# Four pairs by seven products in the last two chunks of an up projection, with the fourth pair's left sums kept in HBM

## The chip, the cores and the metric

The kernel runs on one core of a Trainium2 chip. The metric is the device time of one execution in microseconds, the median of several runs. Beside the times there is a profile of one execution, taken by the hardware profiler.

## The reference

One decoder layer on 256 tokens of width 2048, in float32: a combined input projection, two groups of attention heads, an output projection with a norm and a residual, and then the part that matters here, an MLP with a squared ReLU and a hidden width of 8192:

```python
h = _rmsnorm(x, norm_mlp_pre[layer])
u = jnp.square(jax.nn.relu(h @ w_up[layer]))
x = x + _rmsnorm(u @ w_down[layer], norm_mlp_post[layer])
```

## The kernel before

**Products in three passes.** TensorE gets each float32 operand as two parts: `hi`, the value rounded by ScalarE (L306, L310 with a gain), and `lo`, the rest, by VectorE (L307, L311). A product is three matmuls (hi hi, hi lo, lo hi) of 128 x 128 by 128 x 512. All weights are loaded as `raw` tiles (five buffers) on SP's queue and split into `hi` and `lo` tiles (eight buffers). `Weights.get(i)` emits loads and splits up to six tiles ahead of the one that TensorE is about to use; four ahead around the norm. A load, a split or any other action can be hung in front of a tile by its index (`weights.first`).

**The up projection.** It goes by eight chunks of 1024 columns (`j`, 0 to 7). Within a chunk the 16 blocks of 128 rows (`k0` to `k15`) are taken in the steps of `UP_STEPS`. A step `k` takes one block: both token blocks by both halves of the columns, 12 matmuls. Two neighbouring blocks are a pair, and a pair can be computed by seven block products instead of eight (the Strassen-Winograd form): 21 matmuls instead of 24. This needs sums of the right-hand blocks (the weights) and of the left-hand blocks (the normed activations).

- A step `w` makes the weights' sums on VectorE (`seven`, L359 to L364): `t` and `u` from the two raw tiles in `ab`, which POOL loads; then four splits (b11, b, u, t).
- A step `p` takes weights' sums that were made ahead, by DMA alone, in HBM (`prepare`, L592 to L599): two copies on SP, three accumulating transfers on POOL, and a fourth. They go by the planning clock, one pair after another from 50 us of the plan on, 24 us of the plan for each pair. For chunks 1 to 4 the finished sums come back through POOL into the buffer `tu` (L433); from chunk 5 on, where `tu`'s place holds the output uT8, they come as raw tiles on SP's queue. `PREP` lists the pairs of all `p` steps.
- The left sums of pairs 0 to 3 are made once, in chunk 0 (`left_sums`, L1030 to L1041): pairs 0 to 2 lie in `st`, pair 3 in `st2`. The place of `st2` (tag uT10) is given to the output uT10 in chunk 5. So the first six chunks use four pairs, and chunks 6 and 7 three.

The seven products of all pairs add into the four accumulators of the chunk and into four more banks `m`. After the last pair, `close` (L1072, L1075) makes four closing sums from `m` in the buffer `c`, and `up_evac` adds each to its accumulator (L969) at the chunk's end, applies the ReLU with the norm's scale (`r`, L973), transposes on TensorE (`rt`, L300) and squares into uT (L991).

**Order.** Nothing is scheduled by the compiler. `Flow` keeps a planning clock, to which each matmul adds its expected duration (0.216 us). Chains of work off TensorE are generators that yield the delay until their next part; `flow.pump()`, called after every three matmuls, emits all parts that are due. The clock so fixes the order of instructions on every engine and queue; when they run is decided by semaphores. Each queue is in order: SP's holds raw loads, the stores of x (`xkeep`) and the preparations' copies; POOL's holds the norm's `rstd` operations (L517), the loads of `ab` and `tu`, and the accumulating transfers.

Around the norm between output and up projection (`residual`) the weights run four tiles ahead instead of six; afterwards the buffers are filled again while chunk 0 runs. The last chunk loads the raw tiles of its `w` steps through the five `raw` buffers (but for pair 0), since `ab` holds outputs by then.

Of the kernel before, what the change touches and what calls it, by code (L numbers as in the profile page):

```python
# [18 lines left out]
F32 = mybir.dt.float32  # L19
F32R = mybir.dt.float32r  # L20
# [6 lines left out]
P = 128  # L27
# [18 lines left out]
CW = 1024  # L46
# [50 lines left out]
NUP = FF // CW  # L97


def steps_of(text):  # L100

    return [(s[0], int(s[1:])) for s in text.split()]


UP_STEPS = {0: [("k", k) for k in range(KD)]}
for _j in range(1, 6):
    UP_STEPS[_j] = steps_of("k8 k9 k10 k11 p0 k12 w1 k13 p2 w3 k14 k15")
for _j in range(6, NUP):
    UP_STEPS[_j] = steps_of("k6 k7 k8 k9 k10 w0 k11 k12 w1 k13 w2 k14 k15")
SCALED = {j: range(8) for j in range(1, NUP)}  # L110
PREP = [(j, k) for j in UP_STEPS for w, k in UP_STEPS[j] if w == "p"]
D_PREP = (50.0, 24.0, 12.0)
# [151 lines left out]
def layer(nc, tc, io):  # L264
# [9 lines left out]
    dram = tc.alloc_tile_pool(name="dram", bufs=1, space=bass.MemoryType.DRAM)  # L274
# [69 lines left out]
    late = {}  # L344
# [35 lines left out]
    def seven_up(j, kp):  # L380
        def load():
            if j == FF // CW - 1 and kp:
                return [weights.load(up_weight(j, 2 * kp + i), CW, f"raw_w{j}_{kp}{i}") for i in range(2)]
            return load_two(late["ab"], nc.gpsimd, io["w_up"][2 * kp * P:(2 * kp + 2) * P, j * CW:(j + 1) * CW])

        return seven(load, lambda: [late["up"].tile([P, CW], F32, tag="T", bufs=2, name=f"{n}{j}_{kp}") for n in "tu"])
# [21 lines left out]
    def plan_seven(sums, fs, early, after, more=(), last=(), soon=False):  # L408

        at = max(len(weights.specs) - SUMS_AHEAD, after)  # L410
        if soon:
            more = (*more, (at - max(at - LOAD_AHEAD, after - 2), early))
        for n, f in (*more, (0, sums), *((0, f) for f in last)):
            weights.first.setdefault(at - n, []).append(f)
        return [weights.plan(f) for f in fs], len(weights.specs)
# [3 lines left out]
    wide_u, after, after_p = [], 0, 0  # L419
    for j in range(NUP):  # L420
        wide_u.append([])
        for what, k in UP_STEPS[j]:
            if what == "k":
                g = () if k in SCALED.get(j, ()) else (gcol[:, 8 + k:9 + k],)
                ts = [weights.plan(up_weight(j, k), 1, CW, *g)]
            elif what == "p":
                kept = sums_kept[j, k]
                srcs = [(up_weight(j, 2 * k)[:, :512], 512), (up_weight(j, 2 * k + 1), CW),
                        (kept[:, CW:], CW), (kept[:, :CW], CW)]
                if j < 5:  # L430
                    at = max(len(weights.specs) - 2 * LOAD_AHEAD, after_p)
                    weights.first.setdefault(at, []).append(
                        lambda kept=kept: nc.gpsimd.dma_start(out=late["tu"], in_=kept))  # L433
                    ts = [weights.plan(src, 1, n) for src, n in srcs[:2]] + [weights.plan(
                        lambda hi, lo, o=o: split(hi, lo, late["tu"][:, o:o + CW])) for o in (CW, 0)]
                    after_p = len(weights.specs)
                else:
                    ts = [weights.plan(src, 1, n) for src, n in srcs]
            else:
                ts, after = plan_seven(*seven_up(j, k), after, soon=j < NUP - 1 or k == 0)  # L440
            wide_u[j].append((what, k, ts))

    def down_weight(c, k):
# [14 lines left out]
    for c in range(2):  # L458
        wide_d.append([])
        for what, k in DOWN_STEPS[c]:  # L460
            if what == "k":
                ts = [weights.plan(down_weight(c, k), 1, CW)]
# [558 lines left out]
        tt(out=qs[:, 3], in0=fs[:, 2], in1=qs[:, 2], op=OP.subtract)  # L1021

    sums = []

    def left_sums(kp):

        up, k, tt = late["up"], 2 * kp, nc.vector.tensor_tensor
        f, q = [late["c"][:, i * 512:(i + 1) * 512] for i in range(2)]
        hs = [t[:, k:k + 2, :].rearrange("p k s -> p (k s)") for t in hT]
        tt(out=f, in0=hs[0].bitcast(F32), in1=hs[1].bitcast(F32), op=OP.add)  # L1030
        for i in range(2):
            nc.vector.tensor_scalar_mul(f[:, i * S:(i + 1) * S], f[:, i * S:(i + 1) * S], gcol[:, 8 + k + i:9 + k + i])
        four_sums(q, f)
        sp, i0 = (late["st"], 2 * kp) if kp < 3 else (late["st2"], 2 * kp - 6)
        st = [sp[:, i * 512:(i + 1) * 512] for i in (i0, i0 + 1)]
        yield 3.0
        for t, x in ((hs, f), (st, q)):
            nc.scalar.activation(t[0], x, AF.Copy)
        yield 1.5
        for t, x in ((hs, f), (st, q)):  # L1040
            tt(out=t[1], in0=x, in1=t[0].bitcast(F32), op=OP.subtract)  # L1041
        sums.append([[t[:, i * P:(i + 1) * P] for t in st] for i in range(4)])
        yield 0.5

    def some_sums(kps, after=0.0):
        yield after
        for kp in kps:
            yield from left_sums(kp)
# [20 lines left out]
    def close(c, m):  # L1069

        tt = nc.vector.tensor_tensor
        nc.scalar.activation(c[0], m[1], AF.Copy)  # L1072
        for out, x, y, op in ((1, m[6], c[0], OP.subtract), (2, m[7], c[1], OP.subtract),
                              (1, m[5], c[1], OP.add), (3, c[1], m[7], OP.subtract)):
            tt(out=c[out], in0=x, in1=y, op=op)  # L1075
        return dict(zip(PARTS, c))

    def closing():
        return [late["c"][:, i * 512:(i + 1) * 512] for i in range(4)]
# [3 lines left out]
    for j in range(FF // CW):  # L1083
        at = {bn: 4 * (j % 2) + i for i, bn in enumerate(PARTS)}
        if j == 0:
            accs = {bn: acc_bank(f"acc_u0_{bn[0]}{bn[1]}") for bn in at}
            at = {bn: (turn[0] - 3 + i) % 4 for i, bn in enumerate(at)}
        else:
            accs = {bn: bank(i, f"acc_u{j}_{bn[0]}{bn[1]}") for bn, i in at.items()}
        steps = wide_u[j]  # L1090
        order = in_order(len(steps), (APART[1], 0)) if j == 0 else [(t, b) for t, (w, _, _) in enumerate(steps)
                                                                    for b in range(NB if w == "k" else 1)]
        for t, b in order:
            what, k, tiles = steps[t]
            if (j, t, b) == (0, 8, 0):
                flow.finish(*res)
                late["po"].release()
                mix.release()
                late["up"] = pool("up", "right")
                late["st"] = late["up"].tile([P, 3 * CW], F32R, tag="st", bufs=1, name="st")  # L1100
                for n in ("ab", "c"):
                    late[n] = late["up"].tile([P, 2 * CW], F32, name=n)
                late["st2"] = late["up"].tile([P, CW], F32R, tag="uT10", bufs=1, name="st2")
                late["tu"] = late["up"].tile([P, 2 * CW], F32, tag="uT8", bufs=1, name="tu")
                flow.start(some_sums((0, 1)))
                flow.start(some_sums((2, 3), 18.0))
            if (j, t, b) == (FF // CW - 1, 4, 0):
                weights.limit -= 1
                u_next = split_u(0, 0)
            if what != "k":  # L1110
                flow.until(lambda: len(sums) > k)
            if what == "k":
                w = weights.get(tiles[0])
                h_done(k, b)
                for n in range(2):
                    c = slice(n * 512, (n + 1) * 512)
                    three(accs[b, n], [tok(hT[x], k, b) for x in range(2)], [w[x][:, 0, c] for x in range(2)], t == 0, t == len(steps) - 1)
                    if t == len(steps) - 1:
                        evac.append(flow.start(up_evac(2 * j + n, b, at[b, n], accs[b, n], 0.75 * (2 * b + n),
                                                       more[b, n] if j else None)))  # L1120
                    flow.pump()
                if b == NB - 1:
                    weights.free(tiles[0])
                continue

            pairs = [s[1] for s in steps if s[0] != "k"]
            first, last = k == pairs[0], k == pairs[-1]
            if first:
                m = {n: bank(i, f"m{n}_{j}") for n, i in zip((1, 6, 7, 5), free)}
            blocks = [[tok(hT[x], 2 * k + kk, bb) for x in range(2)] for kk, bb in ((0, 0), (1, 0), (1, 1))]  # L1130
            seven_products(tiles, (blocks, sums[k]), accs, m, first, last)
            if last:
                more = close(closing(), m)
        free = [at[bn] for bn in PARTS]
    u_last = evac[-4:]
# [197 lines left out]
```

## Time and profile before

| | |
|---|---|
| median of 3 runs | 1051.41 us (1051.28 to 1051.68) |
| the profiled execution | 1050.67 us; span 1048.9 us, mean granted TensorE clock 0.998 |
| TensorE matmuls (PE) | 1036.4 us busy, 4844 instructions |
| weight loads into TensorE (PEld) | 863.1 us |
| VectorE (DVE) | 810.6 us |
| ScalarE (ACT) | 633.0 us |
| GpSimd (POOL) | 98.9 us |
| HBM | read 244.18 MB, written 39.32 MB |

A row of the timeline has the start in us from the span's start, the duration, the engine, the line of the kernel, the operation, the tile that it writes and those that it reads, the shape and a count, and in brackets the idle time just before it with what ended it. SPq is SyncE's DMA queue. A row `x3` is several operations merged. A row of the waits has the total in us, the count and the longest. A row of the stretches has for each engine the busy time and the number of instructions.

### The profile page before, as it was taken

The numbers are of one execution on the slowest core, as the hardware profiler recorded it, in microseconds if no ns is written. First come the engines' busy times: TensorE is split into PE (matmuls) and PEld (weight loads), VectorE is DVE, ScalarE is ACT, GpSimd is POOL, SyncE is SP. The second block draws the span as 40 slices with busy tenths as digits, with TensorE's granted clock in tenths as the row PEclk, the third lists the DMA queues.
The fourth block names the chain that finished last, engine by engine and source line by source line (L and its number), as shares of the span: only waits on it lengthen the run. The fifth ranks groups of instructions, "written<-read, shape, count | busy, mean of one in ns | idle before, by whom it ended". The sixth has DMA issues, their size and how long they took to land.

```text
span 1048.9 us, 13584 instructions
## 1 busy us (share of the span) xinstructions
PE 1036.4 (99%) x4844; PEld 863.1 (82%) x4844; DVE 810.6 (77%) x1083; ACT 633.0 (60%) x846; POOL 98.9 (9%) x156
## 2 busy tenths in 40 slices
PE   9999999999999999999999999999999999999996
PEld 7888899888888788888888888888888888888885
DVE  6776546567557669988889798887899988989995
ACT  6675436565545466666756766656567564766661
POOL 0011111112111000010100000000000001112100
PEclk9999999999999999999999999999999999999999
DMA  9999879699878295766766656469778767788952
GB/s 298 369 298 298 221 197 321 197 258 300 227 219 259 84 362 180 281 207 241 262 214 222 228 191 212 139 227 322 249 272 312 267 226 260 264 301 318 368 196 81
DMA packets 93572, 260.81 MB, mean 249 GB/s; under 512 B 8768, under 2 KB 13376, under 8 KB 92096
## 3 DMA queue, kind: packets, MB, share of 16 engines
q1 hardware_dynamic: 71776, 190.61, 52.9%
q0 software_dynamic: 21152, 68.69, 23.0%
q8 instruction: 38, 0.62, 0.2%
q10 hardware_dynamic: 576, 0.64, 0.2%
q14 instruction: 30, 0.25, 0.1%
HBM read 244.18 MB, written 39.32 MB: 270 GB/s over the span
## 4 chain that ended last, share of the span: by engine, by line
PE 87%; DVE 6%; DMA 3%; issue 2%; ACT 2%; POOL 0%; DVEq 0%; POOLq 0%; SPq 0%; ACTq 0%
PE y L296 26%; PE acc_u L296 17%; PE acc_o L296 8%; PE m L296 6%; PE md L296 5%; PE acc_qk L296 4%; PE acc_v L296 4%; PE acc_cq L296 2%; PE acc_ukv L296 2%; PE acc_q L296 2%; PE acc_k L296 2%; DMA raw<-in_w_up 2%; DVE lo L307 2%; PE acc_uq L296 2%; PE acc_ckv L296 1%
## 5 line engine op out<-in xcount | busy, mean ns | idle before, releaser
L307 DVE TENSOR_TENSOR lo<-raw,hi 128x1024 fp32r<-128x1024 f32 (+3 forms) x241 | 269.7, 1137 | 96.3 <-ACT hi L306 95.5
L306 ACT ACTIVATE hi<-raw 128x1024 fp32r<-128x1024 f32 (+3 forms) x241 | 234.7, 988 | 98.0 <-PE y L296 21.5
L296 PE MATMUL y<-hi,uhi 128*128 128x512 f32 x376 | 146.7, 390 | 0.0
L296 PE MATMUL y<-hi,ulo 128*128 128x512 f32 x376 | 146.3, 389 | 0.0
L296 PE MATMUL y<-lo,uhi 128*128 128x512 f32 x376 | 146.3, 389 | 0.0
L296 PE MATMUL acc_u<-hi,hT_hi 128*128 128x512 f32 x356 | 141.7, 398 | 0.0
L296 PE MATMUL acc_u<-hi,hT_lo 128*128 128x512 f32 x356 | 139.2, 391 | 0.4 <-DVE hT_lo L307 0.4
L296 PE MATMUL acc_u<-lo,hT_hi 128*128 128x512 f32 x356 | 138.8, 390 | 0.0
L311 DVE SCALAR_TENSOR_TENSOR lo<-raw,gcol,hi 128x1024 fp32r<-128x1024 f32 x72 | 90.6, 1280 | 16.2 <-ACT hi L310 15.8
L310 ACT ACTIVATE hi<-raw,gcol 128x1024 fp32r<-128x1024 f32 x72 | 81.6, 1149 | 20.3 <-DMA raw<-in_w_up 12.8
L296 PEld LDWEIGHTS y<-hi,ulo 128*128 128x128 f32 x376 | 70.6, 188 | 14.8
L296 PEld LDWEIGHTS y<-hi,uhi 128*128 128x128 f32 x376 | 70.6, 188 | 14.6
L296 PEld LDWEIGHTS y<-lo,uhi 128*128 128x128 f32 x376 | 70.6, 188 | 14.4
L296 PEld LDWEIGHTS acc_u<-hi,hT_lo 128*128 128x128 f32 x356 | 66.8, 188 | 15.0 <-DVE hT_lo L307 0.8
L296 PEld LDWEIGHTS acc_u<-lo,hT_hi 128*128 128x128 f32 x356 | 67.0, 188 | 12.9
L296 PEld LDWEIGHTS acc_u<-hi,hT_hi 128*128 128x128 f32 x356 | 66.9, 188 | 12.9
L296 PE MATMUL m<-hi,st 128*128 128x512 f32 x156 | 56.5, 389 | 0.0
L296 PE MATMUL acc_o<-hi,mixT_hi 128*128 128x512 f32 x128 | 51.8, 405 | 0.0
L307 DVE TENSOR_TENSOR lo<-st_down,hi 128x1024 fp32r<-128x1024 f32 x40 | 48.0, 1220 | 3.9 <-ACT hi L306 3.8
L296 PE MATMUL acc_o<-hi,mixT_lo 128*128 128x512 f32 x128 | 50.2, 392 | 0.0
L296 PE MATMUL acc_o<-lo,mixT_hi 128*128 128x512 f32 x128 | 50.0, 390 | 0.0
L306 ACT ACTIVATE hi<-st_down 128x1024 fp32r<-128x1024 f32 x40 | 42.1, 1052 | 10.8 <-PE y L296 9.4
(331 smaller groups left out, 2037.6 us busy)
## 6 DMA issues: line engine op xcount, KB each, us to landing
raw<-in_w_down SPq DMA_DIRECT2D x88, 512.0 KB, 5.8
raw<-in_w_up SPq DMA_DIRECT2D x86, 512.0 KB, 4.6
raw<-in_w_in SPq DMA_DIRECT2D x55, 512.0 KB, 6.5
raw<-in_w_out SPq DMA_DIRECT2D x32, 512.0 KB, 7.3
ab<-in_w_up POOLq DMA_DIRECT2D x28, 512.0 KB, 5.1
sums<-in_w_up SPq DMA_DIRECT2D x20, 512.0 KB, 7.9
ab_down<-in_w_down POOLq DMA_DIRECT2D x20, 512.0 KB, 6.3
tu<-sums POOLq DMA_DIRECT2D x8, 1024.0 KB, 5.1
```

Source lines behind the costliest of these rows:

```text
L296: nc.tensor.matmul(out, a, b, start=start, stop=stop)
L306: nc.scalar.activation(hi, src, AF.Copy)
L307: nc.vector.tensor_tensor(out=lo, in0=src, in1=hi.bitcast(F32), op=OP.subtract)
L310: nc.scalar.activation(hi, src, AF.Copy, scale=g)
L311: nc.vector.scalar_tensor_tensor(out=lo, in0=src, scalar=g, in1=hi.bitcast(F32), op0=OP.mult, op1=OP.subtract)
```

## The change

Chunks 6 and 7 get the steps of chunks 1 to 5: eight `k` steps and four pairs, of which pairs 0 and 2 are `p` steps. `PREP` grows from ten to fourteen pairs by this. Pair 3's left sums are stored to HBM (`st_kept`) as soon as they are made, on SP's queue. In chunks 6 and 7 they are brought back before the step k11, on SP's queue, into a tile of the buffer `c`, whose closing sums of the chunk before have been used by then; when the last pair is done, the closing sums of the chunk take the buffer again (`new_c`). In chunk 7 no `w` step loads into `ab` any more, and none starts its load early.

```diff
--- before.py
+++ after.py
@@ -103,10 +103,8 @@
 
 
 UP_STEPS = {0: [("k", k) for k in range(KD)]}
-for _j in range(1, 6):
+for _j in range(1, NUP):
     UP_STEPS[_j] = steps_of("k8 k9 k10 k11 p0 k12 w1 k13 p2 w3 k14 k15")
-for _j in range(6, NUP):
-    UP_STEPS[_j] = steps_of("k6 k7 k8 k9 k10 w0 k11 k12 w1 k13 w2 k14 k15")
 SCALED = {j: range(8) for j in range(1, NUP)}
 PREP = [(j, k) for j in UP_STEPS for w, k in UP_STEPS[j] if w == "p"]
 D_PREP = (50.0, 24.0, 12.0)
@@ -437,7 +435,7 @@
                 else:
                     ts = [weights.plan(src, 1, n) for src, n in srcs]
             else:
-                ts, after = plan_seven(*seven_up(j, k), after, soon=j < NUP - 1 or k == 0)
+                ts, after = plan_seven(*seven_up(j, k), after, soon=j < NUP - 1)
             wide_u[j].append((what, k, ts))
 
     def down_weight(c, k):
@@ -1021,6 +1019,13 @@
         tt(out=qs[:, 3], in0=fs[:, 2], in1=qs[:, 2], op=OP.subtract)
 
     sums = []
+    st_kept = dram.tile([P, CW], F32, name="st_kept")
+
+    def new_c(name, dt=F32):
+        return late["up"].tile([P, 2 * CW], dt, tag="c", bufs=1, name=name)
+
+    def parts_of(st):
+        return [[st[:, w * 512 + i * P:w * 512 + (i + 1) * P] for w in range(2)] for i in range(4)]
 
     def left_sums(kp):
 
@@ -1040,6 +1045,8 @@
         for t, x in ((hs, f), (st, q)):
             tt(out=t[1], in0=x, in1=t[0].bitcast(F32), op=OP.subtract)
         sums.append([[t[:, i * P:(i + 1) * P] for t in st] for i in range(4)])
+        if kp == 3:
+            nc.sync.dma_start(out=st_kept, in_=sp.bitcast(F32))
         yield 0.5
 
     def some_sums(kps, after=0.0):
@@ -1098,12 +1105,15 @@
                 mix.release()
                 late["up"] = pool("up", "right")
                 late["st"] = late["up"].tile([P, 3 * CW], F32R, tag="st", bufs=1, name="st")
-                for n in ("ab", "c"):
-                    late[n] = late["up"].tile([P, 2 * CW], F32, name=n)
+                late["ab"], late["c"] = late["up"].tile([P, 2 * CW], F32, name="ab"), new_c("c")
                 late["st2"] = late["up"].tile([P, CW], F32R, tag="uT10", bufs=1, name="st2")
                 late["tu"] = late["up"].tile([P, 2 * CW], F32, tag="uT8", bufs=1, name="tu")
                 flow.start(some_sums((0, 1)))
                 flow.start(some_sums((2, 3), 18.0))
+            if j > 5 and (t, b) == (3, 0):
+                late["st2"] = new_c(f"st2_{j}", F32R)
+                nc.sync.dma_start(out=late["st2"][:, :CW].bitcast(F32), in_=st_kept)
+                sums[3] = parts_of(late["st2"])
             if (j, t, b) == (FF // CW - 1, 4, 0):
                 weights.limit -= 1
                 u_next = split_u(0, 0)
@@ -1130,6 +1140,8 @@
             blocks = [[tok(hT[x], 2 * k + kk, bb) for x in range(2)] for kk, bb in ((0, 0), (1, 0), (1, 1))]
             seven_products(tiles, (blocks, sums[k]), accs, m, first, last)
             if last:
+                if j > 5:
+                    late["c"] = new_c(f"c_{j}")
                 more = close(closing(), m)
         free = [at[bn] for bn in PARTS]
     u_last = evac[-4:]
```

## Prediction

> **What bounds the kernel now.** I read the page first, then who waited for whom on TensorE, the timeline of each engine around the up projection, and the busy time by stretches with the DMA share.
>
> ```profile
> span 1048.9 us, 13584 instructions
> PE 1036.4 (99%) x4844; PEld 863.1 (82%) x4844; DVE 810.6 (77%) x1083; ACT 633.0 (60%) x846; POOL 98.9 (9%) x156
> PE rt L300 <- ACT r L973: 1.2, 3, 0.5
> PE acc_u L296 <- DVE hT_lo L307: 0.4, 1, 0.4
> ```
>
> TensorE is the bound: 1036.4 of 1048.9 us, and of all its waits in the span these two rows are the only ones in the up projection. A matmul taken away is time taken away, as long as VectorE's splits (and behind them ScalarE's and the loads) stay ahead. How far ahead they are differs by stage, and that decides here:
>
> ```profile
> 370.00:390.00 20.00, 20.00 (x92) 16.61 (x91) 11.36 (x15) 12.55 (x18) 2.25 (x4) 1.00 1.01 384
> 390.00:410.00 20.00, 20.00 (x96) 16.50 (x95) 18.56 (x30) 13.73 (x20) 0.00 (x0) 1.00 0.66 215
> 410.00:420.00 10.00, 10.00 (x48) 8.27 (x47) 9.79 (x16) 7.43 (x12) 1.35 (x3) 1.00 0.51 161
> 571.20:614.00 42.80, 42.80 (x199) 35.40 (x198) 36.71 (x39) 29.42 (x34) 2.16 (x4) 1.00 0.71 241
> 614.00:658.40 44.40, 43.88 (x202) 36.05 (x201) 37.20 (x40) 27.26 (x32) 3.23 (x6) 1.00 0.60 191
> 658.40:703.60 45.20, 44.68 (x205) 36.73 (x204) 38.45 (x44) 27.48 (x31) 0.00 (x0) 1.00 0.51 162
> ```
>
> The columns after the stretch are its length, busy time of PE, PEld, DVE, ACT and POOL, then clock, DMA share and GB/s. The last three rows are about chunks 5, 6 and 7: TensorE full, DMA with room. The first three are chunk 0 and the start of chunk 1, right after the norm: the DMA engines are full (1.01) while weight buffers are refilled, and then VectorE is full (18.56 of 20, 9.79 of 10). There is the thin place.
>
> **Part 1, fewer matmuls.** Chunks 6 and 7 go from ten k steps of 12 matmuls and three pairs of 21 (183) to eight and four (180). The pace:
>
> ```profile
> 698.40 0.39 PE L296 MATMUL acc_u<-hi,hT_hi 128*128 128x512 f32 x1
> 703.61 0.39 PE L296 MATMUL acc_u<-hi,hT_lo 128*128 128x512 f32 x1
> ```
>
> These are the first and the last of 24 matmuls without a gap: 5.21 / 23 = 0.2265 us each. Six fewer: -1.36 us, on the bound.
>
> **Part 2, the order at the chunk ends.** Two of TensorE's rt waits stand at the starts of chunks 6 and 7:
>
> ```profile
> 575.35 0.39 PE L296 MATMUL acc_u<-hi,hT_lo 128*128 128x512 f32 x1
> 575.58 0.27 PE L300 MATMUL rt<-ident,r 128*128 128x128 f32 x1
> 618.07 0.39 PE L296 MATMUL acc_u<-hi,hT_lo 128*128 128x512 f32 x1
> 618.98 0.55 PE L300 MATMUL rt<-ident,r 128*128 128x128 f32 x3 [0.52 <-ACT r L973]
> 609.02 1.22 DVE L359 TENSOR_TENSOR t<-ab 128x1024 f32<-128x1024 f32 x1
> 612.80 2.27 DVE L1075 TENSOR_TENSOR c<-m,c 128x512 f32<-128x512 f32 x3
> 573.27 0.69 ACT L973 ACTIVATE r<-acc_u,rstd_pre 128x512 f32<-128x512 f32 x1 [1.16 <-DVE acc_u L969]
> ```
>
> At the start of chunk 5 the transpose follows its matmul by 0.23 us; at chunk 6 by 0.91, 0.68 more, and the same at chunk 7. Before the late one, VectorE does the sums of w0 (three operations from 609.02) ahead of the closing sums (612.80). With the new steps the first pair of chunks 6 and 7 is p0, whose sums are made ahead, as in chunk 5, where r ends at 573.96 and its transpose comes only at 575.58. So -2 x 0.68 = -1.36 us. The closing sums of chunks 6 and 7 now wait for the last matmul that reads the same buffer (`new_c`), some 0.5 to 1 us later; r's slack of 1.6 covers that.
>
> VectorE in chunks 6 and 7: two unsplit k splits and one w's sums go, 3.5 splits come; about even. The loads rise from 8 to 9.5 MB a chunk, plus 0.5 MB to bring the sums back; chunk 5 already runs such p steps at a DMA share of 0.71 with TensorE full. Cost nothing; if that cover fails it is chunk 7, where two raw tiles for each w share five raw buffers with four for each p. The sums' return is issued on SP after chunk start and needed some 25 us later: nothing. Gain of these parts: 2.7 us.
>
> **Part 3, four more prepared pairs.** `PREP` grows from 10 to 14. One preparation is two copies on SP (1 MB, HBM to HBM), 12 us of the plan's clock later three accumulating transfers on POOL (0.75 MB), 12 later a fourth (0.5 MB). The tenth's parts stand in the first three rows below. Counting on by the plan's own clock in the code (24 a pair, which fixes the order of emission and no time), the eleventh's copies follow the tenth's last accumulate; the twelfth's three accumulates fall behind the first rstd_pre; its fourth between the second rstd_pre and the first load of tu; the thirteenth's copies come in SP's queue behind the load of k12 of chunk 0, and its three accumulates between tu and ab. In the trace of before these places are:
>
> ```profile
> 282.66 0.52 SPq L592 DMA_DIRECT2D sums<-in_w_up  x1
> 289.20 0.85 POOL L595 DMA_DIRECT2D sums<-in_w_up  x1 [13.18 <-DMA sums<-in_w_up]
> 321.56 1.20 POOL L599 DMA_DIRECT2D sums<-sums  x1
> 365.79 0.98 POOL L517 TENSOR_TENSOR rstd_pre<-t_pre,neg_half 128x1 f32<-128x1 f32 x1 [3.04 <-DVE t_pre L516]
> 376.84 0.54 POOL L517 TENSOR_TENSOR rstd_pre<-t_pre,neg_half 128x1 f32<-128x1 f32 x1 [10.06 <-DVE t_pre L516]
> 377.52 0.63 POOL L433 DMA_DIRECT2D tu<-sums  x1
> 378.14 1.09 POOL L377 DMA_DIRECT2D ab<-in_w_up  x2
> 368.08 3.51 SPq L188 DMA_DIRECT2D raw<-in_w_up  x5
> 385.91 1.15 ACT L310 ACTIVATE hi<-raw,gcol 128x1024 fp32r<-128x1024 f32 x1 [2.86 <-DMA raw<-in_w_up]
> 387.10 1.28 DVE L311 SCALAR_TENSOR_TENSOR lo<-raw,gcol,hi 128x1024 fp32r<-128x1024 f32 x1 [2.73 <-ACT hi L310]
> 396.20 0.39 PE L296 MATMUL acc_u<-hi,hT_hi 128*128 128x512 f32 x1
> ```
>
> POOL is in order, so the twelfth's accumulates cannot leave before 366.8 and then meet the burst of five loads at 368.08. What they cost the DMA engines, from the stretch 289 to 302, in which the tenth's three are nearly alone:
>
> ```profile
> q0 software_dynamic: 432, 0.79, 40.2%
> ```
>
> 40.2% of 16 engines over 13 us is 5.2 us of all engines for 0.79 MB: 150 GB/s, against 384 in the full stretch above. So ahead of the load of k14 (chunk 0) come 5.2 us of accumulates and 1 MB / 384 GB/s = 2.7 us of copies. The fourth accumulate (0.5 MB at 150, 3.5 us) comes in place of ab (1 MB, 2.7 us), which moves behind the thirteenth's accumulates, and it starts late: +0.8 to -2. With some 0.5 us of free engine time before 368.5, k14's load lands 5.5 us later, my value D. Ends: 8.2 (5.2 + 2.7 + 3.5 - 2.7 - 0.5) and 0, if the SP queue's loads are served before POOL's; 3.3 if the accumulates cost their bytes alone (1.25 MB net / 384 GB/s). I take 5.5 since ScalarE already waits for each of these loads (2.86 before k14), so there is no slack in the loads themselves. k14's split ends at 388.4 and TensorE takes it at 396.20: 7.8 us of cover, which hold. But VectorE is full from there on and carries the delay to where cover is least.
>
> The Trainium skill, "DMA: Bandwidth & Descriptors", section "Queues, rings and completion order", says that a DMA engine goes round the queues that have work, a packet each. In the trace an accumulate's packet takes 0.402 x 16 x 13 us / 432 = 194 ns, so by that rule the POOL queue would hold about half of each engine until its work is done and the sum would stay at +3.3; by bytes alone, with D at 3.3, it would be +1.1. No run here shows the packets' order itself.
>
> The preparations elsewhere: the eleventh and the twelfth's copies run at about 315 to 335, where ScalarE waits for TensorE to free weight buffers (the row below) and for no load: nothing. The norm's rstd on POOL stay ahead of them: nothing. The thirteenth's and fourteenth's later parts delay tu and ab by some 10 us, which chunk 1's p0 and w1 use only after all of chunk 0: nothing.
>
> ```profile
> ACT hi L306 <- PE acc_o L296: 4.8, 3, 1.7
> ACT hi L310 <- DMA raw<-in_w_up: 6.7, 5, 2.9
> ```
>
> (Waits in 320 to 342, and in 368 to 394: total, count, longest.)
>
> **Part 4, the sums kept.** The store of pair 3's sums waits on SP until VectorE has made them, and SP's queue stands:
>
> ```profile
> 400.39 3.33 SPq L188 DMA_DIRECT2D raw<-in_w_up  x3
> 417.00 0.69 DVE L1041 TENSOR_TENSOR st<-c,st 128x512 fp32r<-128x512 f32 x1
> 419.71 1.14 ACT L310 ACTIVATE hi<-raw,gcol 128x1024 fp32r<-128x1024 f32 x1
> 421.62 1.28 DVE L311 SCALAR_TENSOR_TENSOR lo<-raw,gcol,hi 128x1024 fp32r<-128x1024 f32 x1
> 427.15 2.35 DVE L307 TENSOR_TENSOR lo<-tu,hi 128x1024 fp32r<-128x1024 f32 x2
> 431.42 0.39 PE L296 MATMUL m<-hi,st 128*128 128x512 f32 x1
> raw<-in_w_up SPq DMA_DIRECT2D x86, 512.0 KB, 4.6
> ```
>
> In program order the store comes after the load of k12 and ahead of those of chunk 1's k13 and of p2's two (the three from 400.39). They now leave behind 417.69 + 0.35 for the store: 18 us later. k13's lands at 418.05 + 4.6 = 422.65, its splits (1.14, 1.28) end at about 425.2 instead of 422.9: +2.3 us. Least cover follows: the first split from tu for p2 ends at 428.3 and TensorE takes it at 431.42, 3.1 us. Alone, this is hidden. The store itself (0.5 MB, 1.3 us at 384 GB/s) lies ahead of the load, and the fourteenth's accumulates start about then on POOL: 0 to 1.3 + 5.2 / 2 = 3.9 more; I take 1.3.
>
> **The sum.** The delay D shifts 417.69 too, so the terms add: TensorE stands 5.5 + 2.3 + 1.3 - 3.1 = 6.0 us in chunk 1. Less 2.7: +3.3 us. The profiled run took 1050.67 us, 0.74 below the median of the runs; against the median, 1051.41 + 3.3 = 1054.7. Later chunks have more cover and give nothing back.
>
> **Rivals.** (a) Faster: the loads hold their place beside the accumulates. For it: in the first 300 us ten preparations run beside loads and TensorE does not wait. Against: there the buffers are full, here they are refilled. It decides when D and the store's share are under 1.4 (1.4 + 2.3 - 3.1 = 0.6 us of stall, which leaves -2.1); all hidden, 1051.4 - 2.7 = 1048.7. (b) Half hidden: D and the store's share together between 1.4 and 5.6; with D at 3.3 and 0.5 for the store a stall of 3.0, +0.3: 1051.7. (c) The rt waits stay, since closing later takes the place of w0's sums: -1.36 only, 1050.05 with all else hidden. (d) Raw buffers run short in chunk 7 and one w's pair comes late by a landing of 4.6 us, on top of (b): 1056.3. Against it: two w's load that way in chunk 7 already, and TensorE is full there but for the rt wait.
>
> **How the numbers follow.** About 0.2% (2.1 us) can be told from no change. Slower needs a stall above 4.8 us, faster one under 0.6. Forecast 0.45, (d) 0.03: slower 0.48. (b) 0.22 and (c) 0.05: same 0.27. (a) 0.25. The forecast's own range is 1053.5 to 1060.0 (D = 8.2 and 3.9: 11.3 - 2.7 = +8.6). The range over the cases reaches from (a), 1048.5, to 1058.5.
>
> **What would show it.** Right: TensorE waits on VectorE's lo in chunk 1, at about 415 to 440, 3 us or more in all; ScalarE's wait for loads at 368 to 394 grows from 6.7 us to 12 or more; SP shows no raw load for 15 us up to the store of st_kept; the transposes at the starts of chunks 6 and 7 follow without a wait; 1452 matmuls in the up projection. Wrong: TensorE without waits at 370 to 440 (then (a)), or waits of 0.5 us still at chunks 6 and 7 (then (c)).

## The result, and the profile after

| | before | after |
|---|---|---|
| median, same chip | 1051.55 us | 1069.54 us (1068.65 to 1070.75) |
| ratio | | 1.0175 [1.0164, 1.0187] |
| span of the profiled execution | 1048.9 us | 1067.0 us, clock 0.993 |
| TensorE matmuls | 4844 | 4838 |

The change costs 18 us. The forecast was 1054.7 with a range to 1058.5: the direction was right, the size was far outside the range.

The page of the profile after, and the waits of TensorE in 360 to 800 us (before, 1.2 and 0.4 us in all):

```profile
span 1067.0 us, 13640 instructions
PE 1041.6 (98%) x4838; PEld 864.2 (81%) x4838; DVE 810.3 (76%) x1081; ACT 637.2 (60%) x850; POOL 110.9 (10%) x168
PE rt L298 <- ACT r L971: 9.9, 3, 7.1
PE acc_u L294 <- DVE lo L309: 2.2, 3, 0.8
PE acc_u L294 <- DVE c L1082: 1.7, 2, 1.3
PE acc_u L294 <- ACT hi L308: 1.0, 1, 1.0
```

Six matmuls fewer, and yet PE is busy 5.2 us longer: matmuls have become slower somewhere. The same stretches as in the prediction, and two short ones (columns as there):

```profile
370.00:390.00 20.00, 19.07 (x84) 15.27 (x83) 7.37 (x8) 9.03 (x14) 4.43 (x6) 1.00 1.04 329
390.00:410.00 20.00, 15.66 (x67) 12.06 (x66) 13.46 (x21) 10.56 (x12) 2.77 (x4) 1.00 1.05 359
410.00:420.00 10.00, 6.72 (x25) 5.55 (x26) 9.83 (x16) 7.68 (x12) 0.00 (x0) 0.66 0.56 167
413.30:417.80 4.50, 4.50 (x13) 3.73 (x14) 4.36 (x9) 3.44 (x6) 0.00 (x0) 0.50 0.46 164
441.60:445.00 3.40, 3.40 (x9) 2.61 (x9) 2.88 (x3) 3.40 (x5) 0.00 (x0) 0.51 1.07 299
```

Three readings. The DMA engines stay full 20 us longer (1.05 in 390 to 410, where before had 0.66), and in 370 to 390 they move less though they are busy (329 GB/s, before 384). VectorE, full in 390 to 410 before (18.56), has little to split (13.46). And in the last two stretches the clock column is at one half.

**Where the time went, by the start of TensorE's first transpose of a chunk.** In order: chunk 5 and the down projection's start in the trace of after; chunk 2 and the down projection's start in that of before (chunk 5's there is 575.58).

```profile
594.83 0.60 PE L298 MATMUL rt<-ident,r 128*128 128x128 f32 x4
724.51 0.66 PE L298 MATMUL rt<-ident,r 128*128 128x128 f32 x4 [1.36 <-ACT r L971]
```

```profile
447.39 0.66 PE L300 MATMUL rt<-ident,r 128*128 128x128 f32 x4 [0.17 <-ACT r L973]
706.56 0.60 PE L300 MATMUL rt<-ident,r 128*128 128x128 f32 x4
```

Chunk 1's first transpose is at 403.68 before and 413.28 after (rows below): +9.6. Chunk 2's is at 447.39 before (the first row just above) and 466.63 after: +19.24. Chunk 5's: +19.25. The last stretch, chunks 5 to 7, takes 129.68 instead of 130.98: -1.3, with a new wait of 1.36 at its end. So all of the loss lies before the start of chunk 2, in two places.

**Place one, the start of chunk 1.** POOL's and SP's queues after (SPq is SP's):

```profile
366.56 0.87 POOL L593 DMA_DIRECT2D sums<-in_w_up  x1
382.18 1.19 POOL L597 DMA_DIRECT2D sums<-sums  x1
387.52 0.89 POOL L593 DMA_DIRECT2D sums<-in_w_up  x1 [3.53 <-issue]
372.11 0.53 SPq L590 DMA_DIRECT2D sums<-in_w_up  x1
381.28 2.77 SPq L186 DMA_DIRECT2D raw<-in_w_up  x2
```

Then ScalarE and TensorE after:

```profile
395.28 1.15 ACT L308 ACTIVATE hi<-raw,gcol 128x1024 fp32r<-128x1024 f32 x1 [2.61 <-DMA raw<-in_w_up]
411.59 1.06 ACT L304 ACTIVATE hi<-raw 128x1024 fp32r<-128x1024 f32 x1 [1.26 <-DMA raw<-in_w_up]
412.55 0.67 ACT L971 ACTIVATE r<-acc_u,rstd_pre 128x512 f32<-128x512 f32 x1
413.28 1.11 PE L298 MATMUL rt<-ident,r 128*128 128x128 f32 x4 [7.08 <-ACT r L971]
414.62 0.63 PE L294 MATMUL acc_u<-lo,hT_hi 128*128 128x512 f32 x1
415.04 0.63 PE L294 MATMUL acc_u<-hi,hT_lo 128*128 128x512 f32 x1
```

and the same r and transpose before:

```profile
401.46 0.67 ACT L973 ACTIVATE r<-acc_u,rstd_pre 128x512 f32<-128x512 f32 x1
403.68 0.60 PE L300 MATMUL rt<-ident,r 128*128 128x128 f32 x4
```

The r that TensorE waits for needs no load at all: its accumulator is complete. But ScalarE works in the order in which it was given work, and ahead of r stand the splits of chunk 1's first tiles, the last of which waited for its raw tile until 411.59. Before, r ended at 402.13 and its transpose came at 403.68: 1.55 us of cover. After, r starts 11.1 us later, and TensorE stands for 7.08 us.

**Place two, k13 and the end of chunk 1.** SP and POOL, ScalarE, and TensorE after:

```profile
427.31 0.33 SPq L1049 DMA_DIRECT2D st_kept<-st  x1
427.69 2.83 SPq L186 DMA_DIRECT2D raw<-in_w_up  x5
423.32 0.91 POOL L593 DMA_DIRECT2D sums<-in_w_up  x1
438.34 1.15 ACT L308 ACTIVATE hi<-raw,gcol 128x1024 fp32r<-128x1024 f32 x1 [8.99 <-DMA raw<-in_w_up]
458.12 1.15 ACT L308 ACTIVATE hi<-raw,gcol 128x1024 fp32r<-128x1024 f32 x1 [4.89 <-DMA raw<-in_w_up]
439.54 0.50 PE L294 MATMUL acc_u<-hi,hT_hi 128*128 128x512 f32 x1 [1.00 <-ACT hi L308]
440.86 0.50 PE L294 MATMUL acc_u<-lo,hT_hi 128*128 128x512 f32 x1 [0.82 <-DVE lo L309]
466.63 0.66 PE L298 MATMUL rt<-ident,r 128*128 128x128 f32 x4 [1.41 <-ACT r L971]
```

SP holds every raw load behind the store until 427.31; k13's load then goes out together with four others, beside the fourteenth's accumulates (423.32 on POOL), and its split starts 10.6 us after its issue. At the chunk's end a further split waits 4.89 us for its raw tile (458.12); the closing copy stands behind it in ScalarE's order, and TensorE waits for the closing sums (`c`, 1.7 us in all) and for r (1.41 us).

**The account.** Up to 413.28: the wait of 7.08 and two waits on lo of 1.4 together (of the 2.2, less 0.82). From there to chunk 5: waits of 1.00 + 0.82 + 1.7 + 1.41 = 4.9, and matmuls at half clock: eight about 0.43 us apart behind the first wait (414.62, 415.04, and so on) and eight behind the second, each 0.2 us over the normal 0.2265, and the four transposes at 413.28, 1.11 for 0.60: 3.7. Sum 17.1 of 19.25. The remaining 2.1 us stand at the same waits: from start to start of the matmuls, each costs 0.1 to 0.4 us more than the idle time in its row (438.15 to 441.20, across two waits of 1.82 together, is 2.37 us over the pace).

### The profile page after: what moved, and what is told of

Same layout as the page of the kernel before. It is cut to its first block, busy times and chain, and to the rows that moved or that the text cites. A ratio compares the mean times of both kernels' runs of the same rounds, so it can differ in the third digit from the quotient of the medians.

```text
span 1067.0 us, 13640 instructions
## 1 busy us (share of the span) xinstructions
PE 1041.6 (98%) x4838; PEld 864.2 (81%) x4838; DVE 810.3 (76%) x1081; ACT 637.2 (60%) x850; POOL 110.9 (10%) x168
## 4 chain that ended last, share of the span: by engine, by line
PE 84%; DVE 6%; DMA 5%; issue 2%; ACT 2%; SPq 0%; POOL 0%; DVEq 0%; POOLq 0%; ACTq 0%
PE y L294 25%; PE acc_u L294 15%; PE acc_o L294 8%; PE m L294 5%; PE md L294 5%; PE acc_v L294 4%; DMA raw<-in_w_up 4%; PE acc_qk L294 4%; PE acc_ckv L294 2%; PE acc_ukv L294 2%; PE acc_q L294 2%; PE acc_cq L294 2%; PE acc_k L294 2%; DVE lo L305 2%; PE acc_uq L294 2%
## 5 line engine op out<-in xcount | busy, mean ns | idle before, releaser
L305 DVE TENSOR_TENSOR lo<-raw,hi 128x1024 fp32r<-128x1024 f32 (+3 forms) x253 | 282.4, 1133 | 98.5 <-ACT hi L304 97.8
L304 ACT ACTIVATE hi<-raw 128x1024 fp32r<-128x1024 f32 (+3 forms) x253 | 246.0, 985 | 104.1 <-PE y L294 21.2
L294 PE MATMUL acc_u<-hi,hT_hi 128*128 128x512 f32 x344 | 138.6, 403 | 2.8 <-DVE c L1082 1.7
L294 PE MATMUL acc_u<-lo,hT_hi 128*128 128x512 f32 x344 | 136.1, 396 | 2.2 <-DVE lo L309 2.2
L294 PE MATMUL acc_u<-hi,hT_lo 128*128 128x512 f32 x344 | 135.8, 395 | 0.4 <-DVE hT_lo L305 0.4
L294 PEld LDWEIGHTS acc_u<-hi,hT_hi 128*128 128x128 f32 x344 | 65.4, 190 | 16.9 <-DVE c L1082 2.6
L294 PE MATMUL m<-hi,st 128*128 128x512 f32 x168 | 60.8, 389 | 0.0
```

Of the source, the lines that this page charges most:

```text
L294: nc.tensor.matmul(out, a, b, start=start, stop=stop)
L304: nc.scalar.activation(hi, src, AF.Copy)
L305: nc.vector.tensor_tensor(out=lo, in0=src, in1=hi.bitcast(F32), op=OP.subtract)
```

## The experiments

The theory after this reading: the four more preparations cost most, by refilling late; the store costs the rest; the steps of chunks 6 and 7 gain what was forecast. Rivals: that the steps or the sums' return in chunks 6 and 7 cost something, that it is the store's place on SP alone, or that the preparations cost bandwidth anywhere and not an order of waiting at one place. Ratios and differences are against the kernel before, run beside each. In preps_only, copies_only, accum_only and rt_preps nothing uses the added sums, and in the store-only kernels nothing reads the store.

**preps_only.** Before, with the preparations alone.

```diff
+PREP += [(6, 0), (6, 2), (7, 0), (7, 2)]
```

> The kernel before, with four further pairs prepared in HBM (chunks 6 and 7, pairs 0 and 2) that nothing uses; steps, matmuls and buffers are as before. Theory R (the extra preparations take the DMA engines while the weight buffers are refilled after the norm, and the delay runs on through the in-order queues of ScalarE and VectorE): slower by 10 to 18 us, 1062 to 1069, with the wait of about 7 us of TensorE for chunk 0's r at about 405 to 413 and matmuls at 0.43 us behind it. Theory S (SP's queue standing behind the store of the fourth pair's sums is the main cost): there is no store here, at most +4, 1055. Theory C (the buffer of the closing sums and the new steps in chunks 6 and 7): 1051.5.

Measured: 1067.01 us, 1.0153 [1.0139, 1.0167], +16.2. TensorE's waits on r are 8.8 us in all; the one at chunk 1:

```profile
415.85 0.69 PE L301 MATMUL rt<-ident,r 128*128 128x128 f32 x2 [6.37 <-ACT r L974]
```

Place one is the work of the preparations, with no change at chunks 6 and 7.

**store_only.** Before, with the store alone, on SP's queue.

```diff
+        if kp == 3:
+            nc.sync.dma_start(out=st_kept, in_=sp.bitcast(F32))
```

> The kernel before, with the fourth pair's left sums also stored to HBM on SP's queue, and nothing else. Theory R: the raw loads of chunk 1's k13 and p2 leave 17 us later, but land before TensorE needs them, or nearly: 1051.5 to 1053. Theory S: slower by 8 us or more, 1060. Theory C: 1051.5.

Measured: 1056.15 us, 1.0052 [1.0039, 1.0064], +5.3. Expected by the leading theory: at most 1053. The queue, ScalarE's splits of k13's and p2's tiles, VectorE and TensorE:

```profile
417.38 0.33 SPq L1045 DMA_DIRECT2D st_kept<-st  x1
417.75 13.40 SPq L188 DMA_DIRECT2D raw<-in_w_up  x8
423.32 1.15 ACT L310 ACTIVATE hi<-raw,gcol 128x1024 fp32r<-128x1024 f32 x1 [3.90 <-DMA raw<-in_w_up]
428.48 1.06 ACT L306 ACTIVATE hi<-raw 128x1024 fp32r<-128x1024 f32 x1 [2.42 <-DMA raw<-in_w_up]
433.30 2.35 DVE L307 TENSOR_TENSOR lo<-tu,hi 128x1024 fp32r<-128x1024 f32 x2
434.57 0.50 PE L296 MATMUL m<-lo,st 128*128 128x512 f32 x1 [2.06 <-DVE lo L307]
```

So "alone, this is hidden" was false. k13's split starts 3.6 us late (423.32 for 419.71), near the forecast. But I had followed only the first load behind the store: p2's second raw tile is the third of the burst, and its split at 428.48 is 7 us late. Behind it in VectorE's order stands the split of `tu`, which starts at 433.30 instead of 427.15, 6.1 us late against 3.1 of cover: TensorE waits 0.77 us for the raw tile's `lo` and 2.06 for the one from `tu`.

**late.** After, with the last four preparations from 430 us of the plan on.

```diff
-        for jk in PREP:
+        for n, jk in enumerate(PREP):
+            if n == 10:
+                yield max(0.0, 430.0 - flow.clock)
```

> The changed kernel, with the last four preparations put off to 430 us of the plan (chunks 2 to 5) instead of following the first ten at once. Theory R: the waits of chunks 0 and 1 go, only the store on SP's queue stays: 1048.7 to 1051, that is 18 to 21 us less than the changed kernel, and the rt waits at chunks 6 and 7 stay away. Theory S: the loads still stand behind the store: 1060 or more. Theory C: as the changed kernel, 1069.

Measured: 1066.65 us, 1.0146 [1.0130, 1.0161]: a clear miss. Place one is gone (chunk 1's first transpose is at 402.97), place two keeps the store, as in store_only, and the same happens at the ends of chunks 2 to 4, to which the preparations were moved: chunk 2's first transpose is 6.5 us later than before's, chunk 5's 16.9. POOL, ScalarE and TensorE at one of these places:

```profile
526.28 0.92 POOL L593 DMA_DIRECT2D sums<-in_w_up  x1
537.95 1.15 ACT L308 ACTIVATE hi<-raw,gcol 128x1024 fp32r<-128x1024 f32 x1 [7.61 <-DMA raw<-in_w_up]
539.01 0.57 ACT L1081 ACTIVATE c<-m 128x512 f32<-128x512 f32 x1
539.64 0.50 PE L294 MATMUL acc_u<-hi,hT_hi 128*128 128x512 f32 x1 [1.33 <-ACT c L1081]
```

A raw tile is late beside the accumulates, ScalarE waits 7.61 us for it, and the closing copy `c`, which needs no load, stands behind it. So to call the refill alone the thin place was too narrow: here a load that is late at a chunk's end reaches TensorE through ScalarE's order.

**early.** After, with the preparations 17 us of the plan apart, so that all fourteen are issued before the norm.

```diff
-D_PREP = (50.0, 24.0, 12.0)
+D_PREP = (50.0, 17.0, 8.5)
```

> The changed kernel, with all fourteen preparations in the plan's time of the former ten (17 us a pair instead of 24, 8.5 between the parts), so that the last ends about where the tenth ended. Theory R: as with the late ones, 1048.7 to 1051, unless the denser preparations hold up the input projection's loads, which would show as TensorE waits before 300 us (the DMA share is already 0.93 in 0 to 200). Theory S: 1060 or more. Theory C: 1069.

Measured: 1058.0 us, 1.0067 [1.0054, 1.0079], +7.2: a miss too, since theory R had left out what the store costs. Moving the four out of the up projection takes back 10.8 of 18 us. What is left stands mostly at the store: chunk 1's first transpose is 1.2 us later than before's, chunk 2's 7.1. The first is a price in the first 300 us (early_pool).

**copies_only and accum_only.** The preparations taken apart: the two copies of the four pairs on SP alone; and their accumulates on POOL alone (into the sums of one pair, copied once).

```diff
+        if j > 5:
+            yield D_PREP[2]
+            return
```

```diff
-        H, kept = 512, sums_kept[j, kp]
+        H, kept = 512, sums_kept[(6, 0) if j > 5 else (j, kp)]
...
+        if j < 6 or (j, kp) == (6, 0):
             nc.sync.dma_start(out=t, in_=a)
...
```

> The kernel before with the two SP copies of each of the four further preparations, and none of their accumulating transfers. Theory A (the accumulating transfers on POOL's queue, at about 150 GB/s, take the DMA engines in the refill): little is left of the 16 us of the full preparations, 1051 to 1054. Theory Q (the thirteenth's copies stand in SP's own ring ahead of the loads of k13 and k14 of chunk 0): 1058 to 1065.

> The kernel before with the accumulating transfers of four further preparations, all into one scratch area, at the same places of POOL's queue, and only the eleventh's SP copies (at about 315 us). Theory A: most of the 16 us, 1061 to 1067. Theory Q: 1052 to 1057.

Measured: 1055.38 us, 1.0040 [1.0026, 1.0055], +4.3, between the two theories; and 1062.56 us, 1.0104 [1.0091, 1.0117], +11.5, as theory A has it. In sum 15.8 of preps_only's 16.2. One thing differs from the whole preparations: with one scratch area for all, the thirteenth's accumulates wait for the twelfth's fourth and leave at 393.47, in after at 387.52. TensorE's waits on r and the stretch 370 to 390, copies_only first:

```profile
PE rt L301 <- ACT r L977: 6.0, 5, 3.4
370.00:390.00 20.00, 20.00 (x90) 16.54 (x89) 7.32 (x8) 9.55 (x15) 2.25 (x4) 1.00 1.01 385
```

```profile
PE rt L301 <- ACT r L975: 7.5, 4, 5.0
370.00:390.00 20.00, 19.04 (x83) 15.19 (x82) 8.63 (x9) 9.85 (x15) 2.33 (x3) 1.00 0.98 298
```

Beside copies the engines move 385 GB/s, as without them; beside accumulates 298 at the same share. The accumulates (1.25 MB a pair) cost 11.5 us and the copies (1 MB a pair) 4.3, so it isn't the bytes alone. The two also stand at different places of the order, the first accumulates ahead of the five loads and the copies behind them; what of the difference is due to the place, no run shows.

**store_pool.** As store_only, with the store on POOL's queue, where no raw load stands behind it.

```diff
-            nc.sync.dma_start(out=st_kept, in_=sp.bitcast(F32))
+            nc.gpsimd.dma_start(out=st_kept, in_=sp.bitcast(F32))
```

> The kernel before, with the fourth pair's left sums stored to HBM on POOL's queue instead of SP's. If the raw loads that stood behind the waiting store are the whole of the 5.3 us: 1050.8 to 1051.5. If the store's own 0.5 MB beside the loads costs something: 1053 or more.

Measured: 1051.75 us, 1.0003 [0.9994, 1.0011]. The store's 0.5 MB costs nothing that can be measured; its wait at the head of SP's queue was the 5 us.

**rt_preps.** As preps_only, but the transposes of chunk 0 are emitted 2.4 us of the plan later, so that TensorE gets matmuls of chunk 1 ahead of them. No DMA is touched.

```diff
-        yield D_UP if j > 1 else 2 * D_UP
+        yield D_UP if j > 1 else 6.0
```

> The kernel before with four further unused preparations, as in the first of these runs, and the transposes of chunk 0's outputs put 2.4 us of the plan later behind their ReLU. Theory O (ScalarE's in-order queue brings chunk 0's r late, behind splits that wait for loads, and r has under 2 us of cover): TensorE's wait for r falls from 6.4 to about 4 us and the time by 1 to 2.5 us, 1064.5 to 1066. Theory L (TensorE is held by the weight splits themselves, whose cover I had counted): the wait of 6.4 us stays or comes back at the next tile, 1067.

Measured: 1064.61 us, 1.0133 [1.0119, 1.0147], +14.0, so 2.1 us less than preps_only's +16.2; the two intervals just overlap. The same transpose:

```profile
413.05 0.66 PE L301 MATMUL rt<-ident,r 128*128 128x128 f32 x4 [2.64 <-ACT r L974]
```

The wait goes from 6.37 to 2.64. So at this place there were matmuls to run, and r's place in the order held TensorE, as theory O has it. But only about 2 of the 16 us come back: TensorE now also waits 0.85 us for a weight's `lo` ahead of this transpose (at 408.30) and 1.31 us for a square behind it (426.72). How much r's order is of the whole loss, this run leaves open.

**early_pool, mid_pool.** early with the store on POOL; and the same with 18.5 us between pairs.

> The changed kernel with the fourteen preparations in the former ten's time and the store of the fourth pair's sums on POOL's queue. With both causes gone: 5.3 us below the early one, 1052.7. What it then stands above the kernel before, less the gain of 2.7, is the price of denser preparations in the first 300 us (about 4.5). If chunks 6 and 7 themselves cost time: 1056 or more, with TensorE waits after 600 us.

> As the early one with the store on POOL's queue, but 18.5 us of the plan for a pair, so that the last accumulating transfer falls behind the first rstd_post, into the stretch around 349 to 360 in which the DMA share is 0.3. With fewer transfers at once before 200 us than at 17: the waits of 1.8 and 1.7 us at 95 and 181 us shrink, 1050 to 1052.

Measured: 1052.59 us, 1.0015 [1.0006, 1.0024]; 1051.78 us, 1.0010 [1.0002, 1.0019]. TensorE's waits of early_pool, then of mid_pool:

```profile
PE pT_a L298 <- DVE s_a L661: 1.8, 1, 1.8
PE acc_cq L294 <- ACT ckv L753: 1.7, 1, 1.7
```

```profile
PE pT_a L298 <- DVE s_a L661: 2.0, 1, 2.0
```

Both repair places one and two: between 372 and 448 us TensorE has no wait of 0.15 us or more, and at chunk 2's start r still costs 1.3 and 0.5 us. What is gained at chunks 6 and 7 is then paid in the attention part, where denser preparations delay loads in the same way: before has no wait on s_a and one of 0.7 us on ckv. In 60 to 200 us ScalarE waits 23.4 us for raw tiles in early_pool and 18.0 in mid_pool, 8.6 before, and early_pool's ckv stands behind a split that waited 2.50 us for its tile. Of mid_pool's forecast the time came, but the wait on s_a did not shrink.

**w_steps.** The steps of chunks 6 and 7 by VectorE's sums, with no further preparation, and the store on POOL.

```diff
-    UP_STEPS[_j] = steps_of("k8 k9 k10 k11 p0 k12 w1 k13 p2 w3 k14 k15")
+    UP_STEPS[_j] = steps_of("k8 k9 k10 k11 p0 k12 w1 k13 p2 w3 k14 k15" if _j < 6 else
+                            "k8 k9 k10 k11 k12 w0 k13 w1 k14 w2 w3 k15")
```

> The changed kernel without further preparations: in chunks 6 and 7 all four pairs take their weights' sums on VectorE (steps k8 k9 k10 k11 k12 w0 k13 w1 k14 w2 w3 k15), and the store goes on POOL's queue. No preparation beyond the ten, so no wait in chunks 0 and 1: 1050 (1.36 less) if VectorE keeps up, which has 2.6 us more work for each w and is 85% busy there; 1053 to 1056 if the last pair, followed by one k step only, brings the closing sums late.

Measured: 1062.85 us, 1.0110 [1.0095, 1.0126], +12.3, above both forecasts. Its longest wait in the up projection:

```profile
PE acc_u L295 <- ACT c L1080: 3.4, 1, 3.4
```

This closing copy (665.15) stands behind a split that waited 3.10 us for its raw tile (664.10): the same order again. With this order of the steps, four `w` pairs in a chunk cost more than their matmuls save; another order was not tried.

**best.** After, the store on POOL, the first three preparations 24 us apart and the rest 17, and chunk 7's pairs earlier, so that its closing is done in time.

```diff
+            yield from prepare(*jk, 12.0 if n < 3 else 8.5)
...
+    UP_STEPS[_j] = steps_of("k8 k9 k10 k11 p0 k12 w1 k13 p2 w3 k14 k15" if _j < 7 else
+                            "k8 k9 k10 p0 k11 w1 k12 p2 w3 k13 k14 k15")
```

> As the last one (17 us of the plan for a pair, store on POOL's queue), but with 24 us for each of the first three pairs and 17 after them, so that the start is as in the kernel before; and in chunk 7 the pairs one k step earlier, so that three k steps follow the last. If the wait of 2.0 us for the heads' probabilities at 92 us comes from the denser preparations and the wait of 1.1 us for r at 706 us from the late closing of chunk 7, both go: 1048.6 to 1050, 1 to 2 us less than before. If the later, denser ones (0.9 to 1.0 DMA share in 100 to 340) bring a wait of their own, 1050 to 1052.

Measured: 1051.76 us, 1.0006 [0.9997, 1.0015]: no different from before. Transposes at the starts of chunk 5 and of the down projection:

```profile
580.39 0.60 PE L299 MATMUL rt<-ident,r 128*128 128x128 f32 x4
708.58 0.60 PE L299 MATMUL rt<-ident,r 128*128 128x128 f32 x4
```

Chunks 5 to 7 take 128.19 us instead of 130.98: 2.79 less, the forecast's 2.7. It is lost again further ahead: chunk 1's first transpose is 2.9 us later than before's, with a wait of 1.2 us on ckv (0.7 before), and chunk 2's 4.8, with a wait of 1.4 us on r; the rest was not traced. No version beat the kernel before.

## Why the prediction was wrong

**Right: parts 1 and 2, the gain of 2.7 us.** best shows 2.79, and in after the transposes at the starts of chunks 6 and 7 follow without a wait. In after itself the gain is 1.3, since chunk 7's closing ends late and a wait of 1.36 stands at the down projection's start. I had let r's slack of 1.6 us cover a later closing; in chunk 6 it does, where the closing copy starts as soon as `m` is complete (672.30). In chunk 7 the copy starts 1.7 us after the last matmul into `m` (714.60 + 0.39), behind splits of the down projection's tiles that wait for their loads:

```profile
715.76 1.06 ACT L304 ACTIVATE hi<-raw 128x1024 fp32r<-128x1024 f32 x1 [0.70 <-DMA raw<-in_w_down]
716.73 0.57 ACT L1079 ACTIVATE c<-m 128x512 f32<-128x512 f32 x1
```

It is place one's order in small. Rival (d) had looked at chunk 7's loads, but for a pair that comes late, and no such wait appeared.

**Right: the order in the queues.** The twelfth's accumulates leave at 366.56, right behind the first rstd_pre (366.8 by the trace of before), its fourth at 382.18 between the second rstd_pre and tu, the thirteenth's copies at 372.11 behind k12's load. The next raw load is at 381.28. Rivals (a) and (b), hidden or half hidden, fell. Of the signs, SP's queue shows no raw load from 408.11 to the store, and ScalarE's wait for loads at 368 to 394 is 11.8 us; but in chunk 1 TensorE waits on `lo` for 0.82 us only, and its long wait is for r.

**Wrong in size: D.** k14's split starts at 395.28 instead of 385.91: 9.4 us, above the 5.5 taken and its upper end of 8.2. The terms show it when they are taken apart. In copies_only k14's split is 4.3 us late (390.16), where the sum had 2.7. In accum_only it is 6.4 us late (392.28), where the sum had 2.7 to 5.5 for three accumulates and the fourth, less the free time. In after the thirteenth's accumulates (387.52) had also left while k14's load was under way, and my sum counted them behind it; but accum_only has its 6.4 us before they leave (393.47), so the difference doesn't need them.

**The step that failed: "least cover follows: ... 3.1 us", at p2.** I looked for cover only between a weight tile's split and TensorE. The least cover was elsewhere: r of chunk 0, 1.55 us ahead of its transpose, in the same in-order queue of ScalarE as the splits that wait for loads. A delay of 9.4 us in the loads delayed r by 11.1 us and stopped TensorE for 7.08 us, with weights at hand: the next wait for a weight comes at 439.54. rt_preps, which moves only these transposes and the squares behind them, shortens the wait from 6.37 to 2.64 us and bears this out; that r's order is the whole of the loss, it does not show. In the forecast's terms: it put no stall ahead of chunk 1's first transpose, where 9.6 us were lost, and 6.0 in chunk 1, where 9.6 were. The trace of before had both rows (401.46 and 403.68): I had listed the splits of ScalarE there, and not all that it does.

**Failed: "Alone, this is hidden", in part 4.** store_only costs 5.3 us, store_pool none that can be measured. The hold on SP moved three loads, and I priced the first. The third's split is 7 us late, and with it the one from `tu`, 6.1 against 3.1 of cover. In after, with the preparations beside them, k13's split is 18.6 us late (438.34 for 419.71); the sum had 5.5 + 2.3 + 1.3 = 9.1.

**Missing: the clock.** The sum priced every matmul at 0.2265 us. Behind the 7.08 us wait and the pair at 439.54 and 440.86 the granted clock was 0.50 and 0.51, and sixteen matmuls and four transposes took 3.7 us more: stalls cost more than their length. The Trainium skill, "TensorE: Matmul & The Clock Gate", section "Part 1: The HAM clock gate (the "warmup" mystery)", says that the clock drops to 4/8 after a free-running window of about 3.4 us that counts as idle, and comes back after a busy one. The trace agrees behind the long wait: 0.50 for 4.5 us. Behind waits of 1.00 and 0.82 us, with single matmuls in between, the clock was halved just the same (PE was busy for 1.58 of the 3.40 us from 438.20 on), so here the window need not have been wholly idle.

**By the sum.** Forecast +6.0 of stall - 2.7 = +3.3. The runs give: copies 4.3, accumulates 11.5, store 5.3, chunks 6 and 7 -2.7: 18.4, against 18.0 measured; with the -1.3 that after itself shows it is 19.8. Each is known to about 1.4 us, so they add within that; why they do was not tried. The range didn't follow its own working either: the forecast's upper end was 1060.0 and rival (a) 1048.7, and the range was given as 1048.5 to 1058.5. The measured 1069.54 lies outside both.

## What to carry to other kernels

Before a DMA is added next to full loads, look in the trace for the work with the least cover in every in-order queue that waits for these loads: an evacuation or a closing copy that stands behind a waiting split has the split's delay with none of its cover. A DMA that waits for data belongs on a queue with nothing urgent behind it, and every load that it holds back has to be followed, not the first alone. A stall of TensorE is to be priced with the slow clock behind it.

## What the runs showed of the hardware

- Beside accumulating transfers from HBM to HBM the DMA engines moved fewer bytes at the same share: 298 GB/s in a stretch with them (share 0.98) against 385 beside plain copies (1.01).
- The granted clock fell to 0.51 for 3.4 us behind two waits of 1.00 and 0.82 us close together, not only behind the wait of 7.08 us (0.50).
